# Stick-breaking attention in a hybrid decoder layer: carried sums folded to 64 rows, memory's norm taken by token, queries and keys split in 128 rows

## The chip, the cores and the metric

The kernel runs on one core of one Trainium2 chip. The metric is device time in microseconds (us) of one execution. The kernel before has a median of 851.5 us over three runs.

## The reference, cut to what matters

One layer, 512 tokens, width 1024, all in float32. The part that the change touches is the causal stick-breaking attention (8 heads of 64) and the norm of the 256 memory tokens:

```python
def rms_norm(x, g):
    var = jnp.mean(x * x, axis=-1, keepdims=True)
    return x * lax.rsqrt(var + EPS) * g

# stick-breaking attention: A[t,s] = sigmoid(z_ts) * prod_{s<j<t} (1 - sigmoid(z_tj)), z = q.k / sqrt(64), s < t
z = einsum('bhqd,bhkd->bhqk', qb, kb) * scale
log_fail = where(mask, log_sigmoid(-z), 0)
log_later = cumsum(log_fail, axis=3, reverse=True) - log_fail
weights = where(mask, exp(log_sigmoid(z) + log_later), 0)
out = einsum('bhqk,bhkd->bhqd', weights, vb)

# later, in the memory sublayer
m = rms_norm(mem, norm_mem_kv)          # 256 memory tokens
kv = m @ w_mem_kv
```

Around it stand the short convolution branch, the merge gates, the output projection, the memory cross-attention, a SwiGLU FFN and a final norm.

## The kernel before

Every product of float32 matrices is made of three products of float32r operands: an operand is split into a rounded part "hi" (a cast on ScalarE) and the remainder "lo" (a subtraction on VectorE), and hi*hi, hi*lo and lo*hi are added in PSUM (`mm3`, L154 to L156). A weight block of 128 columns is loaded by SyncE's queue into one of four `wr` buffers (L141), cast to `wh` (L149) and its remainder written to `wl` (L150). `gemm` then runs 24 matmuls of 512 columns.

**Attention.** Keys lie on partitions, queries on columns. The 8 heads are 4 pairs p; for each pair the key tiles kt = 3, 2, 1, 0 are swept (16 steps), with 128, 256, 384 and 512 query columns per head. `scores` (L408) makes z on TensorE, ScalarE makes softplus of it (Abs, Exp, Ln: L415 to L417; VectorE closes it, L418), GpSimd cuts the diagonal block (`causal`, L376), and the result e, the negative log of failing, is split in hi and lo (`l`, L390 and L391). e then gets the sum of all later key tiles added (L430) and is split once more (`r`): this running sum is carried into the next key tile. `weights` adds to z, in PSUM, first the carried sum (a matmul of each of the two parts of `r` with a 128x128 matrix of -1, L448) and then the sums inside the tile (parts of `l` with a triangle of -1, L451); ScalarE takes Exp (L453), GpSimd cuts the diagonal, VectorE scales and splits (`ah`, `al`, L457 and L458), and `values` multiplies with v (L470) one step later. For kt = 3 the carried sum is `l` itself and no `r` is made.

Between these pieces stands the filler: for each pair the projections of the next pair's q and k (`qk_part`), three projections of the convolution, and some gates, each one `gemm` of 24 matmuls. Scores of step i+1 are put in the middle of step i's filler; step i ends with `weights` of i and `values` of i-1. Some splits are deferred to the end of a step (`settle_behind`) and may not run before the last Exp of that step on ScalarE. A scheduler then sets the order of each engine's instructions, and each engine and each queue runs its own in order.

**q and k.** With two heads stacked on 128 partitions, k is held per head as hi in one half of the partitions and lo in the other; q is held per head as hi in both halves and lo in both halves. One matmul over 128 partitions then adds two of the products. Before, each half is cast and subtracted by itself (64 rows, L310, L313, L318, L322), and q's halves are copied across by four DMAs (L327).

**Memory's norm.** The transposed memory is loaded in four pieces during steps 1, 3, 5, 7 (L486), squared on ScalarE (L493), summed over its 8 tiles on GpSimd (L496, L498), split on VectorE (L184, L185), averaged over partitions by two matmuls (L190), and turned into the factors by a row of length 256 on ScalarE and VectorE; one row of it goes through DRAM on GpSimd's queue to give the same factors one per partition.

Of the kernel before, what the change touches and what calls it, by code (L numbers as in the profile page):

```python
# [21 lines left out]
MEM = 256  # L22
# [5 lines left out]
NJ = NF // 2  # L28
EPS = 1e-6
MEM_AT = (1, 3, 5, 7)  # L30
MEAN_AT = 13
EARLY = 2
WARM = 8
FIRST = 4
# [6 lines left out]


@with_exitstack
def hybrid_layer(ctx: ExitStack, tc: tile.TileContext, xT_d, memT_d, cols_d, wv_d, win_d,
                 wbr_d, wmix_d, wmq_d, wmk_d, wmv_d, wmo_d, wfi_d, wfo_d, gfin_d, out):
    nc = tc.nc

# [19 lines left out]
    def unit(s, cols=512):  # L67
        return upool.tile([P, cols], F32R, tag="u", name=nm(s), padded_shape=[P, 512])

    def tmp(s, cols=512):  # L70
        return tpool.tile([P, cols], F32, tag="t", name=nm(s), padded_shape=[P, 512])

    def f(ap):
        return ap.bitcast(F32)
# [228 lines left out]
        while behind:  # L303
            behind.pop(0)(*last)

    def qk_parts(p, i, t, last):
        if i:
            ks[p] = [unit("k") for _ in range(2)]
            for h, hs in enumerate(HALVES):
                casts.append(nc.scalar.copy(ks[p][h][hs, :], t[hs, :]))  # L310
                after(casts[-1], last)
            for h, hs in enumerate(HALVES):
                after(nc.vector.tensor_tensor(out=ks[p][h][HALVES[1 - h], :], in0=t[hs, :],  # L313
                                              in1=f(ks[p][h][hs, :]), op=ALU.subtract), last)
            return
        qs[p] = [[unit("q") for _ in range(2)] for _ in range(2)]
        for h, hs in enumerate(HALVES):
            casts.append(nc.scalar.copy(qs[p][h][0][hs, :], t[hs, :]))  # L318
            after(casts[-1], last)
        for h, hs in enumerate(HALVES):  # L320
            hi, lo = qs[p][h]
            after(nc.vector.tensor_tensor(out=lo[hs, :], in0=t[hs, :], in1=f(hi[hs, :]),  # L322
                                          op=ALU.subtract), last)
        for part in range(2):
            for h, hs in enumerate(HALVES):
                q = f(qs[p][h][part])
                nc.sync.dma_start(q[HALVES[1 - h], :], q[hs, :])  # L327

    gates = {}

# [54 lines left out]

    rest, later = {}, {}

    def lsplit(t, n, tag, bufs):
        hi, lo = (lpool.tile([P, n], F32R, tag=tag, name=nm(tag), bufs=bufs) for _ in range(2))
        nc.scalar.copy(hi, t)  # L390
        nc.vector.tensor_tensor(out=lo, in0=t, in1=f(hi), op=ALU.subtract)  # L391
        return hi, lo

    def part_of(parts, hs, some, n):

# [3 lines left out]
    def scores(p, kt):  # L399
# [11 lines left out]
        for hs, bank in zip(heads_of(kt), zs[p, kt]):  # L411
            w = len(hs) * n
            z = bank[:, :w]
            e = tmp("e")[:, :w]
            nc.scalar.activation(e, z, AF.Abs)  # L415
            nc.scalar.activation(e, e, AF.Exp, scale=-1.0)
            nc.scalar.activation(e, e, AF.Ln, bias=1.0)  # L417
            nc.vector.scalar_tensor_tensor(out=e, in0=z, scalar=0.0, in1=e, op0=ALU.max,  # L418
                                           op1=ALU.add)
            causal(by_head(e, n))  # L420
            bufs = 4 // len(hs)
            sp[p, kt, hs] = lsplit(e, w, f"l{kt}", bufs)
            if kt == TT - 1:
                later[hs] = e
                rest[p, kt - 1, hs] = sp[p, kt, hs]
            elif kt > 0:
                t = by_head(e, n)[:, :, P:]
                before = heads_of(kt + 1)[0] if len(heads_of(kt + 1)) == 1 else hs
                old = by_head(part_of([later[before]], before, hs, n - P)[0], n - P)
                nc.vector.tensor_tensor(out=t, in0=t, in1=old, op=ALU.add)  # L430
# [52 lines left out]
    accm = tmp("accm", MEM)  # L483

    def load_mem(k2, t):
        nc.sync.dma_start(t, memT_d[2 * k2 * P:(2 * k2 + 2) * P, :].rearrange("(j p) t -> p j t",  # L486
                                                                              p=P))

    def mem_square(k2):

        mk = f(unit("mk")).rearrange("p (j t) -> p j t", j=2)
        load_mem(k2, mk)
        nc.scalar.activation(mk, mk, AF.Square)  # L493
        for j in range(2):
            if k2 + j == 0:
                nc.gpsimd.tensor_copy(accm, mk[:, j, :])  # L496
            else:
                nc.gpsimd.tensor_tensor(out=accm, in0=accm, in1=mk[:, j, :], op=ALU.add)  # L498

    fill = []  # L500
    for p in range(TT):
# [804 lines left out]
def _layout(x, mem, norm_mix, w_in, conv_w, w_branch_a, w_branch_b, w_mix_out, norm_mem_q,  # L1306
# [12 lines left out]
    def by_pair(w):  # L1319
# [8 lines left out]
    arrays = {  # L1328
        "xT": x[0].T,
        "memT": mem[0].T,  # L1330
        "columns": columns.T,
        "w_value": by_row(w_in[0][:, O_V:O_V + SBW]),
        "w_in": by_column(w_in[0]),
# [30 lines left out]
```

## Time and profile before

| | |
|---|---|
| three runs | 851.5 us median, 851.43 to 852.21 |
| profiled execution | 850.78 us, its span 849.1 us, granted TensorE clock 0.998 |
| TensorE busy | 838.4 us, 99% of the span, 4778 matmuls in the trace |
| VectorE / ScalarE / GpSimd busy | 656.2 / 458.4 / 159.7 us |
| attention and its filler | about 28 to 196 us of the span |

The span runs from the first to the last instruction; the execution is 1.7 us longer. A matmul's row in the profile is longer than the distance to the next one, because matmuls are pipelined: the row's length includes the way through the array. What a matmul costs in a stream is therefore read from the starts of neighbouring rows, and a stall shorter than that tail shows as a larger distance of starts, not as idle time. PE is TensorE, DVE VectorE, ACT ScalarE, POOL GpSimd, SP SyncE, and a q behind a name is that engine's queue of DMA issues.

### The profile page before, as it was taken

How to read it: one execution, taken by the hardware profiler on the slowest of the kernel's cores; microseconds unless marked ns; L12 is line 12 of the kernel's file. 1: busy time of each engine (PE TensorE's matmuls, PEld its weight loads, DVE VectorE, ACT ScalarE, POOL GpSimd, SP SyncE). 2: the span in 40 equal slices, each digit the busy share in tenths (PEclk: the TensorE clock that was granted, in tenths of full speed). 3: DMA queues.
4: the chain of work that ended last, by engine and by line, in shares of the span. 5: the costliest groups of instructions: out<-in, count | busy, mean ns of one | idle time of the engine just before them, and what ended most of it. 6: DMA issues, size and time to landing. Idle time of an engine off the chain costs nothing.

```text
span 849.1 us, 12662 instructions
## 1 busy us (share of the span) xinstructions
PE 838.4 (99%) x4778; PEld 737.8 (87%) x4778; DVE 656.2 (77%) x1043; ACT 458.4 (54%) x810; POOL 159.7 (19%) x171
## 2 busy tenths in 40 slices
PE   9999999999999999999999999999999999999996
PEld 7888887888888899888888789999999999888885
DVE  7869989896766586587455679888887888999786
ACT  7567767474333344444444556655555555576664
POOL 0013221120566640163000101111111110000001
PEclk9999999999999999999999999999999999999999
DMA  8542232225588765566431335767767772465552
GB/s 298 156 142 64 93 117 75 75 76 183 200 310 309 297 245 190 174 230 247 151 81 49 112 75 142 181 174 187 186 176 187 190 186 85 155 221 196 171 187 99
DMA packets 50510, 141.62 MB, mean 167 GB/s; under 512 B 5521, under 2 KB 7569, under 8 KB 47634
## 3 DMA queue, kind: packets, MB, share of 16 engines
q1 hardware_dynamic: 40818, 105.93, 36.7%
q0 software_dynamic: 9344, 34.62, 15.7%
q8 instruction: 37, 0.61, 0.3%
q10 hardware_dynamic: 288, 0.28, 0.1%
q14 instruction: 23, 0.19, 0.1%
HBM read 125.07 MB, written 13.64 MB: 163 GB/s over the span
## 4 chain that ended last, share of the span: by engine, by line
PE 95%; DVE 3%; ACT 1%; issue 0%; DMA 0%; POOL 0%; SPq 0%; ACTq 0%
PE z L817 15%; PE p L1083 11%; PE y L817 7%; PE pr L154 7%; PE pr L155 7%; PE pr L156 7%; PE v L817 4%; PE r L156 3%; PE r L154 3%; PE r L155 3%; PE v L272 3%; PE mq L156 2%; PE mq L154 2%; PE br L155 2%; PE br L154 2%; PE mq L155 2%
## 5 line engine op out<-in xcount | busy, mean ns | idle before, releaser
L149 ACT CAST wh<-wr 128x1024 fp32r<-128x1024 f32 x84 | 88.0, 1052 | 151.7 <-issue 70.9
L150 DVE TENSOR_TENSOR wl<-wr,wh 128x1024 fp32r<-128x1024 f32 x84 | 110.6, 1318 | 37.0 <-ACT wh L149 36.9
L154 PE MATMUL pr<-xgh,wh 128*128 128x512 f32 x288 | 112.7, 391 | 0.0
L155 PE MATMUL pr<-xgl,wh 128*128 128x512 f32 x288 | 112.3, 390 | 0.0
L156 PE MATMUL pr<-xgh,wl 128*128 128x512 f32 x288 | 112.3, 390 | 0.0
L552 POOL TENSOR_TENSOR pre<-pre 128x512 f32<-128x512 f32 x44 | 72.1, 1642 | 31.4 <-DMA pre<-in_w_ffn_out_dram 29.1
L786 POOL DMA_DIRECT2D ws<-in_w_ffn_in_dram x22 | 26.5, 1207 | 258.4 <-DVE wf L807 104.7
L817 PE MATMUL z<-xdh,wf 128*128 128x256 f32 x352 | 70.5, 283 | 0.2 <-ACT sb L838 0.2
L156 PEld LDWEIGHTS pr<-xgh,wl 128*128 128x128 f32 x288 | 54.1, 188 | 11.5
L154 PEld LDWEIGHTS pr<-xgh,wh 128*128 128x128 f32 x288 | 54.1, 188 | 10.6
L155 PEld LDWEIGHTS pr<-xgl,wh 128*128 128x128 f32 x288 | 54.1, 188 | 10.3
L838 ACT COPY sa<-z 128x256 f32<-128x256 f32 x44 | 16.4, 373 | 79.2 <-PE z L817 79.1
L817 PEld LDWEIGHTS z<-xdh,wf 128*128 128x128 f32 x352 | 57.3, 189 | 0.5 <-ACT sb L838 0.4
L807 DVE TENSOR_TENSOR wf<-s,wf 128x512 fp32r<-128x512 f32 x44 | 30.3, 691 | 26.0 <-ACT wf L806 25.8
L817 PE MATMUL z<-xdl,wf 128*128 128x256 f32 x176 | 49.8, 283 | 0.0
L898 DVE TENSOR_TENSOR wl<-wr,wh 128x1024 fp32r<-128x1024 f32 x33 | 40.3, 1220 | 4.4 <-ACT wh L965 4.2
L965 ACT CAST wh<-wr 128x1024 fp32r<-128x1024 f32 x33 | 34.6, 1049 | 7.0 <-DMA wr<-sums 3.3
L817 PE MATMUL z<-xch,wf 128*128 128x256 f32 x176 | 35.4, 284 | 0.1
L817 PE MATMUL v<-xoh,wf 128*128 128x256 f32 x176 | 35.4, 283 | 0.0
L817 PE MATMUL y<-xch,wf 128*128 128x256 f32 x176 | 35.4, 283 | 0.0
L817 PE MATMUL z<-xf,wf 128*128 128x256 f32 x264 | 35.4, 283 | 0.0
L817 PE MATMUL y<-xoh,wf 128*128 128x256 f32 x176 | 35.3, 283 | 0.0
(337 smaller groups left out, 2403.3 us busy)
## 6 DMA issues: line engine op xcount, KB each, us to landing
wr<-in_w_in_dram SPq DMA_DIRECT2D x36, 512.0 KB, 3.3
pre<-in_w_ffn_out_dram POOLq DMA_DIRECT2D x11, 1024.0 KB, 8.0
sums<-pre POOLq DMA_DIRECT2D x11, 1024.0 KB, 5.0
ws<-in_w_ffn_in_dram SPq DMA_DIRECT2D x22, 512.0 KB, 3.7
wg<-in_w_ffn_in_dram SPq DMA_DIRECT2D x22, 512.0 KB, 4.0
ws<-in_w_ffn_in_dram POOLq DMA_DIRECT2D x22, 512.0 KB, 6.4
wr<-sums SPq DMA_DIRECT2D x22, 512.0 KB, 3.9
wr<-in_w_ffn_out_dram SPq DMA_DIRECT2D x16, 512.0 KB, 3.5
```

Of the source, the lines that this page charges most:

```text
L149: after(nc.scalar.copy(h2, raw), lead[-1:])
L150: lows.append(nc.vector.tensor_tensor(out=l2, in0=raw, in1=f(h2), op=ALU.subtract))
L154: nc.tensor.matmul(ps, a[0], b[0], start=start, stop=False, **kw)
L155: nc.tensor.matmul(ps, a[0], b[1], start=False, stop=False, **kw)
L156: nc.tensor.matmul(ps, a[1], b[0], start=False, stop=stop, **kw)
L552: nc.gpsimd.tensor_tensor(out=t[:, a, :], in0=t[:, a, :], in1=t[:, b, :], op=ALU.add)
L786: nc.gpsimd.dma_start(s13, a[:, 0:4:3, :], accum_op=ALU.add)
L807: nc.vector.tensor_tensor(out=w[:, 1, :], in0=raw, in1=f(w[:, 0, :]), op=ALU.subtract)
L817: nc.tensor.matmul(ps[:, :HS], a, b, start=i < 3 and k == 0 and j == 0, stop=k == KP - 1 and j == 2, skip_group_check=True)
L898: nc.vector.tensor_tensor(out=lo, in0=src, in1=f(hi), op=ALU.subtract)
L965: nc.scalar.copy(hi, raw)
L1083: nc.tensor.matmul(res[i][s2], a[:, ts], b, start=j == 0 and n == 0, stop=n == 2 and j == (BEHIND - 1 if (i, s2) == (5, 1) else NJ - 1))
```

## The change

Three edits. First, `rests`: the sum of the two halves of the partitions of e is taken before it is split. The carried matmul has -1 everywhere, so it only sums over partitions; the upper 64 rows are copied down by a DMA and added to the lower 64, the sum's hi goes to rows 0 to 63 and its lo to rows 64 to 127 of one tile, and one matmul instead of two carries it (for kt = 2 and 1; kt = 3 stays). It is deferred to the end of the step. Second, q and k of pairs 1 to 3 are cast and subtracted in full height, and DMAs move the halves (6 for q, 3 for k; the last ones overwrite what the first ones read). Third, the memory is loaded by token, ScalarE's square sums along the row, the factors are made on 128x2 numbers, and go through DRAM to be spread over all partitions. The place where this ends is step 9 instead of 13.

```diff
-MEAN_AT = 13
+MEAN_AT = 9
...
+    def qk_parts(p, i, t, last):
+        if p == 0:
+            return qk_halves(p, i, t, last)
+        low, high = HALVES
+        hi, lo, other = unit("qk"), unit("qk"), unit("qk")
+        casts.append(nc.scalar.copy(hi, t))
+        after(casts[-1], last)
+        after(nc.vector.tensor_tensor(out=lo, in0=t, in1=f(hi), op=ALU.subtract), last)
+        if i:
+            moves = (other, low, hi, high), (other, high, lo, high), (hi, high, lo, low)
+            ks[p] = [hi, other]
+        else:
+            rest = unit("qk")
+            moves = [(b, to, a, high) for a, b in ((hi, other), (lo, rest)) for to in HALVES]
+            moves += [(a, high, a, low) for a in (hi, lo)]
+            qs[p] = [[hi, lo], [other, rest]]
+        for a, to, b, at in moves:
+            nc.sync.dma_start(f(a)[to, :], f(b)[at, :])
...
+    def rests(p, kt, hs, e, w, last):
+        low, high = HALVES
+        t = tmp("rf")[:, :w]
+        nc.sync.dma_start(t[low, :], e[high, :])
+        nc.vector.tensor_tensor(out=t[low, :], in0=t[low, :], in1=e[low, :], op=ALU.add)
+        r = lpool.tile([P, w], F32R, tag=f"r{kt}", name=nm("r"), bufs=2 // len(hs))
+        after(nc.scalar.copy(r[low, :], t[low, :]), last)
+        nc.vector.tensor_tensor(out=r[high, :], in0=t[low, :], in1=f(r[low, :]), op=ALU.subtract)
+        rest[p, kt - 1, hs] = r,
...
                 later[hs] = e
-                rest[p, kt - 1, hs] = lsplit(e, w, f"r{kt}", bufs)
+                behind.append(lambda *last, e=e, w=w, hs=hs: rests(p, kt, hs, e, w, last))
...
-    def mem_square(k2):
-        mk = f(unit("mk")).rearrange("p (j t) -> p j t", j=2)
-        load_mem(k2, mk)
-        nc.scalar.activation(mk, mk, AF.Square)
-        for j in range(2):
-            if k2 + j == 0:
-                nc.gpsimd.tensor_copy(accm, mk[:, j, :])
-            else:
-                nc.gpsimd.tensor_tensor(out=accm, in0=accm, in1=mk[:, j, :], op=ALU.add)
+    def mem_square(i):
+        h, t = divmod(i, MT)
+        mk = f(unit("mk"))
+        nc.sync.dma_start(mk, mem_d[t, :, h * 512:(h + 1) * 512])
+        nc.scalar.activation(mk, mk, AF.Square, scale=D ** -0.5, accum_out=ms[:, i:i + 1])
+
+    def mem_factors():
+        var = spool.tile([P, MT], F32, tag="mv", name="mv", bufs=1)
+        nc.vector.tensor_tensor(out=var, in0=ms[:, :MT], in1=ms[:, MT:], op=ALU.add)
+        rm = rstd_of(var, MT, "rm")
+        d = dpool.tile([1, MEM], F32, tag="rm", name="rmd")
+        nc.gpsimd.dma_start(d.rearrange("o (t p) -> p (o t)", p=P), rm)
+        rmb = cpool.tile([P, MEM], F32, tag="rmb", name="rmb")
+        nc.gpsimd.dma_start(rmb, d.broadcast_to([P, MEM]))
+        return rm, rmb
...
-        if i == MEAN_AT - 4:
-            mean = squares_mean(accm, MT)
         if i == MEAN_AT:
-            rmb = mean[0]("rmb")
-            rm = turned_row(rmb[0:1, :], MT, "rm", nc.gpsimd, nc.gpsimd)
+            rm, rmb = mem_factors()
```

The scheduler moves instructions with it. In the rows below a number behind a name is a buffer's; line numbers of the changed kernel are its own (L478 is the former L448, L481 the former L451, L410 and L421 the former L391, L418 the new addition of the halves).

TensorE, pair 0, `weights` of kt = 1: z_611 and z_614 (now z_613 and z_616) are the two heads' scores, r the carried sum, l the tile's own. Before:

```order
L448 MATMUL z_611<-r_542,neg_91 128x256
L448 MATMUL z_611<-r_543,neg_91 128x256
L451 MATMUL z_611<-l_623,negtri 128x384
L448 MATMUL z_614<-r_542,neg_91 128x256
L448 MATMUL z_614<-r_543,neg_91 128x256
```

Now:

```order
L478 MATMUL z_613<-r_580,neg_91 128x256
L481 MATMUL z_613<-l_625,negtri 128x384
L481 MATMUL z_613<-l_626,negtri 128x384
L478 MATMUL z_616<-r_580,neg_91 128x256
L481 MATMUL z_616<-l_636,negtri 128x384
L481 MATMUL z_616<-l_637,negtri 128x384
```

One matmul per head takes the place of two, here and at kt = 0 of every pair.

VectorE, pair 2, from the convolution's product to the second half of the weights of kt = 2 (al_1491, now al_1499). Before:

```order
L348 TENSOR_TENSOR cu_1475<-pr_1450,r0b_363 128x512
L391 TENSOR_TENSOR r_1426<-e_1414,r_1425 128x384
L349 TENSOR_TENSOR cu_1475<-cu_1475,gc_1406 128x512
L391 TENSOR_TENSOR r_1441<-e_1429,r_1440 128x384
L351 TENSOR_SCALAR cv_1479<-cu_1475,gcol 128x512
L150 TENSOR_TENSOR wl_1726<-wr_1723,wh_1725 128x1024
L355 SCALAR_TENSOR_TENSOR cv_1479<-cu_1475,gcol,cv_1479 128x512
L457 TENSOR_SCALAR ah_1490<-a_1487,r_372 128x512
L355 SCALAR_TENSOR_TENSOR cv_1479<-cu_1475,gcol,cv_1479 128x512
L458 SCALAR_TENSOR_TENSOR al_1491<-a_1487,r_372,ah_1490 128x512
```

Now:

```order
L367 TENSOR_TENSOR cu_1483<-pr_1458,r0b_363 128x512
L150 TENSOR_TENSOR wl_1738<-wr_1735,wh_1737 128x1024
L368 TENSOR_TENSOR cu_1483<-cu_1483,gc_1422 128x512
L370 TENSOR_SCALAR cv_1487<-cu_1483,gcol 128x512
L374 SCALAR_TENSOR_TENSOR cv_1487<-cu_1483,gcol,cv_1487 128x512
L487 TENSOR_SCALAR ah_1498<-a_1495,r_372 128x512
L374 SCALAR_TENSOR_TENSOR cv_1487<-cu_1483,gcol,cv_1487 128x512
L488 SCALAR_TENSOR_TENSOR al_1499<-a_1495,r_372,ah_1498 128x512
L418 TENSOR_TENSOR rf_1508<-rf_1508,e_1430 64x384
L418 TENSOR_TENSOR rf_1514<-rf_1514,e_1441 64x384
L421 TENSOR_TENSOR r_1511<-rf_1508,r_1511 64x384
L448 SCALAR_TENSOR_TENSOR e_1545<-z_1539,e_1545 128x512
```

The two splits of the carried sum stood ahead of al; their additions and splits now stand behind it.

VectorE, a few instructions later in pair 2, where the weights of kt = 1 are split (heads 0 and 1). Before:

```order
L391 TENSOR_TENSOR l_1542<-e_1535,l_1541 128x512
L457 TENSOR_SCALAR ah_1567<-a_1564,r_372 128x384
L458 SCALAR_TENSOR_TENSOR al_1568<-a_1564,r_372,ah_1567 128x384
L457 TENSOR_SCALAR ah_1578<-a_1575,r_372 128x384
L458 SCALAR_TENSOR_TENSOR al_1579<-a_1575,r_372,ah_1578 128x384
L174 TENSOR_TENSOR yl_1587<-gb_1557,yh_1586 128x512
```

Now:

```order
L410 TENSOR_TENSOR l_1562<-e_1555,l_1561 128x512
L487 TENSOR_SCALAR ah_1586<-a_1583,r_372 128x384
L150 TENSOR_TENSOR wl_1804<-wr_1801,wh_1803 128x1024
L488 SCALAR_TENSOR_TENSOR al_1587<-a_1583,r_372,ah_1586 128x384
L487 TENSOR_SCALAR ah_1596<-a_1593,r_372 128x384
L448 SCALAR_TENSOR_TENSOR e_1632<-z_1627,e_1632 128x256
L488 SCALAR_TENSOR_TENSOR al_1597<-a_1593,r_372,ah_1596 128x384
```

A weight split (wl) and the next pair's softplus (e) now stand between the last l and the second head's al.

More of the change, by code (lines that the diff above doesn't have):

```diff
@@ L43, in hybrid_layer @@
 @with_exitstack
-def hybrid_layer(ctx: ExitStack, tc: tile.TileContext, xT_d, memT_d, cols_d, wv_d, win_d,
+def hybrid_layer(ctx: ExitStack, tc: tile.TileContext, xT_d, memT_d, mem_d, cols_d, wv_d, win_d,
                  wbr_d, wmix_d, wmq_d, wmk_d, wmv_d, wmo_d, wfi_d, wfo_d, gfin_d, out):
@@ L304, in settle_behind, with qk_halves @@
             behind.pop(0)(*last)
-    def qk_parts(p, i, t, last):
+    def qk_halves(p, i, t, last):
         if i:
@@ L386, in hybrid_layer, with lsplit @@
     rest, later = {}, {}
-    def lsplit(t, n, tag, bufs):
+    def lsplit(t, n, tag, bufs, last=()):
         hi, lo = (lpool.tile([P, n], F32R, tag=tag, name=nm(tag), bufs=bufs) for _ in range(2))
-        nc.scalar.copy(hi, t)
+        after(nc.scalar.copy(hi, t), last)
         nc.vector.tensor_tensor(out=lo, in0=t, in1=f(hi), op=ALU.subtract)
         return hi, lo
+    def rests(p, kt, hs, e, w, last):
[7 more added lines that the diff above has]
+        rest[p, kt - 1, hs] = r,
     def part_of(parts, hs, some, n):
@@ L481, in values @@
             oT.append(split(t, "o"))
-    accm = tmp("accm", MEM)
     def load_mem(k2, t):
@@ L487, in load_mem @@
                                                                               p=P))
[L489 to L498 removed]
+    ms = cpool.tile([P, 2 * MT], F32, tag="ms", name="ms")
+    def mem_square(i):
[12 more added lines that the diff above has]
+        return rm, rmb
     fill = []
@@ L1330, in _layout @@
         "memT": mem[0].T,
+        "mem": mem[0].reshape(MT, P, D),
         "columns": columns.T,
```

## The prediction

> **What bounds the kernel now.** I read the page's busy shares and its chain first, then the busy time by stretch (last row: stretch, its length, busy us of PE, PEld, DVE, ACT and POOL with their instructions, granted clock, DMA):
>
> ```profile
> PE 838.4 (99%) x4778; PEld 737.8 (87%) x4778; DVE 656.2 (77%) x1043; ACT 458.4 (54%) x810; POOL 159.7 (19%) x171
> PE 95%; DVE 3%; ACT 1%; issue 0%; DMA 0%; POOL 0%; SPq 0%; ACTq 0%
> 28.00:196.00 168.00, 167.04 (x791) 140.06 (x790) 141.71 (x231) 111.09 (x202) 36.90 (x62) 1.00 0.32 103
> ```
>
> TensorE is busy nearly everywhere, and 95% of the chain that ended last is TensorE. In the attention (28 to 196 us), the only stage that the change touches, it is busy 167.04 of 168 us. So a matmul that goes is worth its place in the stream, and an instruction on another engine costs only where TensorE comes to wait for it. VectorE, busy 141.71 of those 168 us, is the engine closest behind.
>
> "Busy" hides short stalls, since a matmul's row reaches 0.2 us past the start of the next one. So I went along the starts of TensorE's rows in the timeline of this stage and looked for distances over the usual one. The usual ones (two 256-column matmuls take 0.24 us of the stream, two of 384 take 0.35; one of 512 takes 0.23, the last two rows):
>
> ```profile
> 64.41 0.40 PE L448 MATMUL z<-r,neg 128*128 128x256 f32 x2
> 64.65 0.34 PE L451 MATMUL z<-l,negtri 128*128 128x384 f32 x1
> 77.76 0.51 PE L448 MATMUL z<-r,neg 128*128 128x384 f32 x2
> 78.11 0.62 PE L451 MATMUL z<-l,negtri 128*128 128x512 f32 x2
> 78.57 0.51 PE L448 MATMUL z<-r,neg 128*128 128x384 f32 x2
> ```
>
> And the places where TensorE really stood, in the same columns (start, length, what):
>
> ```profile
> 65.06 0.28 PE L470 MATMUL o<-ah,v 128*128 128x256 f32 x1
> 65.39 0.39 PE L470 MATMUL o<-al,v 128*128 128x256 f32 x1
> 122.98 0.40 PE L470 MATMUL o<-ah,v 128*128 128x512 f32 x1
> 123.32 0.50 PE L470 MATMUL o<-al,v 128*128 128x512 f32 x1
> 139.22 0.61 PE L408 MATMUL z<-q,k 128*128 128x512 f32 x2
> 140.37 0.73 PE L408 MATMUL z<-q,k 128*128 128x512 f32 x2 [0.53 <-ACT a L453]
> 140.94 0.39 PE L154 MATMUL pr<-xgh,wh 128*128 128x512 f32 x1
> 144.86 0.28 PE L470 MATMUL o<-ah,v 128*128 128x256 f32 x1
> 145.51 0.39 PE L470 MATMUL o<-al,v 128*128 128x256 f32 x1 [0.38 <-DVE al L458]
> ```
>
> Against those distances the first two rows lose 0.33 - 0.12 = 0.2 us, the next two 0.34 - 0.23 = 0.1 us; from 139.22 to 140.94 stand 1.72 us for four matmuls of 0.23, 0.8 us lost; from 144.86 to 145.51 0.65 us for one of 0.12, 0.5 us lost. In sum 1.6 us of stalls. All but the one at 139 stand ahead of a product with al, the last of VectorE's pieces.
>
> **What leaves TensorE.** The groups of the carried-sum matmul with two parts:
>
> ```profile
> L448 PE MATMUL z<-r,neg 128*128 128x384 f32 x16 | 4.1, 337 | 0.0
> L448 PE MATMUL z<-r,neg 128*128 128x256 f32 x16 | 3.2, 281 | 0.0
> ```
>
> The order of the changed kernel keeps one of each two: 8 of 384 columns at 0.35 / 2 = 0.175 us and 8 of 256 at 0.24 / 2 = 0.12 us go: 1.40 + 0.96 = 2.36 us. The length in the rows (337, 281 ns) would be the wrong price, for most of it lies under the next matmul. The Trainium skill (TensorE: Matmul & The Clock Gate, Back-to-back issue gap) gives a sustained spacing of 131 ns at 512 columns and 81 ns at 128; an estimate between them (98 and 114 ns) would make this term 1.7 us and the forecast 848.9. This trace does not agree: it shows 0.23 us at 512 columns, so that rule gets no weight in the sum.
>
> Memory's norm had two matmuls in the stream, with their waits around them:
>
> ```profile
> 168.88 0.39 PE L154 MATMUL pr<-xgh,wh 128*128 128x512 f32 x1
> 169.21 0.39 PE L190 MATMUL varb<-acch,mean_r 128*128 128x256 f32 x1
> 169.55 0.40 PE L155 MATMUL pr<-xgl,wh 128*128 128x512 f32 x1
> ```
>
> From 168.88 to 169.55 are 0.67 us where 0.23 would stand: 0.44 us go. Both together: **2.8 us off TensorE's stream**, all other matmuls staying.
>
> **What moves on the other engines, and what of it reaches TensorE.** Prices from the groups of the attention (count, busy us, mean ns) and the landing of q's copies:
>
> ```profile
> L322 DVE TENSOR_TENSOR q<-qk,q 64x512 fp32r<-64x512 f32 x8 | 5.5, 683 | 0.1
> L391 DVE TENSOR_TENSOR r<-e,r 128x384 fp32r<-128x384 f32 x8 | 4.7, 587 | 0.6 <-ACT r L390 0.6
> L391 DVE TENSOR_TENSOR r<-e,r 128x512 fp32r<-128x512 f32 x4 | 2.7, 678 | 0.2 <-ACT r L390 0.2
> L310 ACT CAST k<-qk 64x512 fp32r<-64x512 f32 x8 | 4.9, 618 | 0.1
> DMA to landing us min/median/max: 2.2/2.3/5.3
> ```
>
> 64 rows cost what 128 rows cost (683 against 678 ns). So full-height q and k save two of four VectorE operations and two of four casts per pair, for three pairs: 6 x 0.68 = 4.1 us of VectorE, 6 x 0.62 = 3.7 us of ScalarE. The fold adds one VectorE addition per carried sum, 4 of 512 and 8 of 384 columns: 4 x 0.68 + 8 x 0.59 = 7.4 us; its casts and subtractions stay in number and length. GpSimd loses the eight operations of memory's sum, VectorE six of 256 columns (at most 0.43 us each, the row of accl below: 2.6 us), and gets five on two columns, below that price. VectorE ends within 1 or 2 us of its old sum: how much does not decide, only where.
>
> Where it matters is pair 2, around the stalls at 139 and 145. The chain of waits there is VectorE's:
>
> ```profile
> 133.09 0.70 DVE k L313
> 133.81 0.43 DVE accl L185
> 139.80 0.47 DVE r L391
> 140.87 0.68 DVE r L391
> 144.72 0.75 DVE al L458
> ```
>
> Out of it go one of k's two subtractions (0.70), the memory's split (0.43), and the two r (1.15), which the new order puts behind al; into it come the addition and the subtraction of kt = 2's fold (2 x 0.68). That is 0.9 us less ahead of al. This stretch also began late:
>
> ```profile
> 118.52 1.99 POOL L498 TENSOR_TENSOR accm<-accm,mk 128x256 f32<-128x256 f32 x2 [2.07 <-ACT mk L493]
> 120.79 0.49 DVE L457 TENSOR_SCALAR ah<-a,r 128x512 fp32r<-128x512 f32 x1 [1.69 <-POOL a L376]
> ```
>
> The diagonal of pair 1's last weights waited behind two memory additions on GpSimd, and VectorE 1.69 us for it. Without them that start can come up to 1.69 us sooner; I take 1.3, since memory's square and two tiny steps now stand between ScalarE's pieces there. Against it TensorE itself reaches 139 us sooner: by 1.2 us of removed matmuls (two pairs) and by the two small stalls, 1.5 us in all. So the 1.3 us at 139 and 145 change by 1.5 - 0.9 - 1.3, to 0.6; those at 65 and 123 (0.3 us), which stand behind memory's square or additions, go. Bounds: none of the 1.6 us saved, all of it saved. I take 1.0 us saved.
>
> What comes new: behind al VectorE now does the two r and two additions, 4 x 0.59 = 2.4 us, then a weight split and an e, before the second head's next al:
>
> ```profile
> 151.84 0.62 DVE L458 SCALAR_TENSOR_TENSOR al<-a,r,ah 128x384 fp32r<-128x384 f32 x1
> 154.06 0.33 PE L470 MATMUL o<-al,v 128*128 128x384 f32 x1
> ```
>
> That al ended at 152.46; its matmul started at 154.06, 1.6 us later; the path to it is now longer and TensorE's need sooner. I charge 0.5 us, bounds 0 and 1.5.
>
> **Waits that come new.** The fold's copy waits on SyncE's queue for e, and behind it stand weight loads; k's and q's last copies wait until the first ones have landed (2.3 us), with the same loads behind them. A load and its cast are far apart:
>
> ```profile
> 59.15 0.34 SPq L141 DMA_DIRECT2D wr<-in_w_in_dram  x1
> 86.03 1.05 ACT L149 CAST wh<-wr 128x1024 fp32r<-128x1024 f32 x1 [0.59 <-PE pr L155]
> ```
>
> 27 us for this one, so two landings' time in the queue is hidden. On VectorE the addition waits for the copy's landing, with e, l and al queued behind it. The folded sum of pair 0, kt = 2 shows the room:
>
> ```profile
> 53.66 0.41 DVE L430 TENSOR_TENSOR e<-e,e 128x256 f32<-128x256 f32 x1
> 54.99 0.68 DVE L391 TENSOR_TENSOR r<-e,r 128x512 fp32r<-128x512 f32 x1
> ```
>
> e stands at 54.07, r was done at 55.67, and the first L448 that reads it starts at 64.41: 8.7 us, of which a copy (2.3) and an addition (0.68) take 3. In pairs 1 to 3 at least one gemm of 24 matmuls (5.4 us at 0.23) stands between as well. The row through DRAM moves to a place where GpSimd's next select is due; it holds GpSimd from the one DMA's issue to its landing. I count these waits at 0; the upper bound is the slower rival.
>
> **Sum.** -2.8 - 1.0 + 0.5 = -3.3 us. Against the profiled execution (850.78 us, span 849.1) that is 847.5. It ran 0.7 us under the median of 851.5, so the forecast for the median is **848.2 us**. What follows the attention keeps its order and its TensorE stream, so the gain should reach the end.
>
> **Rivals.** (1) VectorE swallows it: TensorE comes earlier to pair 2, but VectorE's pieces there do not, so that what was saved before 145 us (4 x 0.12 + 4 x 0.175 + 2 x 0.12 = 1.4 us) turns into longer waits for al and no stall is won: -2.8 + 1.4 = -1.4, 850.1 us. For it: the chain above is VectorE's from 133 to 145 us. Against it: the 1.69 us wait on GpSimd at its head goes. (2) Slower, by one mechanism: the copies land late and VectorE, in order, stands at the fold's addition while e, l and al queue behind. With a landing of 5.3 instead of 2.3 us it stands 3.0 us per pair of heads; it decides where two steps follow each other within a gemm or two (pairs 0 and 2): 2 x 3.0 = 6.0 us against 3.3, 854.2 us. It turns the sign once these waits exceed 3.3 us in all. For it: one copy of q did land in 5.3 us. Against it: the median is 2.3. (3) All stalls go and none comes: -2.8 - 1.6 = -4.4, 847.1 us. (4) The fold does not thin the stream, because TensorE's next operand is late anyway: the waits on TensorE (0.5 and 0.4 us named) are too few for that; it falls together with rival 1.
>
> **Chances and range.** Forecast 66%, rival 1 (with 4) 15%, rival 2 7%, rival 3 12%. A change of under 0.2% (1.7 us) cannot be told from none: forecast and rival 3 are faster, but for a small part of the forecast whose stalls come out on the bad side (none saved, 1.5 new: -1.3): faster 0.79; within 0.2% 0.14 (rival 1 without its worst end); slower 0.07. The range from 846.4 (rival 3 and 0.7 us, the spread of the runs) to 850.6 us (past rival 1) leaves out rival 2.
>
> **What would show it.** Right: 18 matmuls fewer; L478 with 16 folded matmuls, each followed at 0.12 or 0.175 us; the 1.99 us of GpSimd ahead of pair 1's last select gone; the distances around 65 and 123 us at their usual size; a smaller one at 139 and 145, a new one near 151. Wrong: VectorE idle ahead of `rf`, waiting for a DMA; al waits that add up to more than 1.6 us; or an idle TensorE at the start of a pair, waiting for q's or k's last copy.

## The result, and the profile after

| | before | changed |
|---|---|---|
| median | 851.46 us (851.07 to 852.21, 6 runs) | 858.19 us (856.72 to 859.65, 6 runs) |
| ratio | | 1.0078, 95% interval 1.0068 to 1.0088 |
| profiled execution, its span | 850.78, 849.1 us | 856.72, 855.0 us |
| matmuls in the trace | 4778 | 4760 |

The changed kernel is 6.7 us **slower**. The forecast was 848.2 us (846.4 to 850.6), and slower had a chance of 0.07.

First the page's busy shares and the attention's row of the busy time by stretch (stretch, length, busy us of PE, PEld, DVE, ACT and POOL, granted clock, DMA), as shown of before:

```profile
PE 838.3 (98%) x4760; PEld 737.0 (86%) x4760; DVE 656.9 (77%) x1048; ACT 455.2 (53%) x808; POOL 150.2 (18%) x163
28.00:196.00 168.00, 161.50 (x750) 135.31 (x749) 139.58 (x233) 104.98 (x196) 26.91 (x54) 0.98 0.37 112
```

Eighteen matmuls are gone, as announced, and TensorE is still as busy in sum (838.3 us), because some matmuls now last longer. In the attention it is busy 161.50 of 168 us where it was 167.04, and the clock's mean is 0.98 instead of 1.00. The groups of the folded matmul, and TensorE's rows at the two places that used to stall near 65 and 123 us:

```profile
L478 PE MATMUL z<-r,neg 128*128 128x384 f32 x8 | 2.7, 338 | 0.0
L478 PE MATMUL z<-r,neg 128*128 128x256 f32 x8 | 2.2, 277 | 0.0
65.39 0.28 PE L500 MATMUL o<-ah,v 128*128 128x256 f32 x1
65.50 0.28 PE L500 MATMUL o<-al,v 128*128 128x256 f32 x1
121.51 0.40 PE L500 MATMUL o<-ah,v 128*128 128x512 f32 x1
121.74 0.40 PE L500 MATMUL o<-al,v 128*128 128x512 f32 x1
```

The starts are 0.11 and 0.23 us apart: both stalls have gone, and up to here the run goes as predicted, about 1.6 us ahead of before. Then, in pair 2, TensorE's rows:

```profile
134.61 0.27 PE L500 MATMUL o<-al,v 128*128 128x128 f32 x1
139.26 0.79 PE L154 MATMUL pr<-xgh,wh 128*128 128x512 f32 x1 [4.38 <-DVE gc L361]
140.71 0.63 PE L154 MATMUL pr<-xgh,wh 128*128 128x512 f32 x1
141.99 0.63 PE L154 MATMUL pr<-xgh,wh 128*128 128x512 f32 x1
144.55 1.28 PE L438 MATMUL z<-qk,qk 128*128 128x512 f32 x4
149.34 0.28 PE L500 MATMUL o<-ah,v 128*128 128x256 f32 x1
149.94 0.39 PE L500 MATMUL o<-al,v 128*128 128x256 f32 x1 [0.33 <-DVE al L488]
155.12 0.66 PE L438 MATMUL z<-qk,qk 128*128 128x128 f32 x4 [1.79 <-ACT a L483]
```

TensorE stands for 4.5 us ahead of the convolution's gemm (L154); such idle time on TensorE is called a hole below. Then three matmuls take 1.28 us (140.71 to 141.99), 0.427 us each, where 0.23 is usual: from 139.26 to 144.55 twelve matmuls take 5.29 us instead of 2.76, which loses 2.5 us more. At 149.34 another 0.5 us and at 155.12 another 1.8 us are lost. The busy time by stretch shows the clock behind it:

```profile
134.60:139.20 4.60, 0.28 (x3) 0.14 (x2) 1.84 (x4) 1.69 (x4) 0.00 (x0) 0.88 0.51 153
139.20:144.50 5.30, 5.24 (x12) 4.13 (x13) 4.69 (x10) 4.54 (x9) 0.59 (x2) 0.50 0.41 127
```

The granted clock is 0.50 behind the hole; below, this is called the half clock. So 4.5 + 2.5 + 0.5 + 1.8 = 9.3 us are lost, and 2.8 us of matmuls and the 1.6 us of old stalls are won: +4.9 us. The span grew by 5.9 us; 1.0 us of it I cannot assign. Most of that lies behind the attention: the matmul of the carried sum at 189.10 us of before starts at 194.30 us now, 5.2 us later.

What TensorE waited for, followed back, begins on GpSimd. Its rows of that time, then the rows of SyncE's queue (start, length, what):

```profile
121.14 0.74 POOL L532 DMA_DIRECT2D rmd<-rm  x1 [3.43 <-DVE rm L129]
121.90 0.43 POOL L395 TENSOR_SCALAR_AFFINE_SELECT e<-e 128x256 f32<-128x256 f32 x1
129.66 0.57 POOL L534 DMA_DIRECT2D rmb<-rmd  x1 [7.33 <-DMA rmd<-rm]
130.24 0.42 POOL L395 TENSOR_SCALAR_AFFINE_SELECT a<-a 128x256 f32<-128x256 f32 x1
```

```profile
119.17 10.90 SPq L346 DMA_DIRECT2D qk<-qk  x6
130.16 2.38 SPq L141 DMA_DIRECT2D wr<-in_w_in_dram  x1
132.64 0.46 SPq L417 DMA_DIRECT2D rf<-e  x1
```

And the landing of q's and k's moves:

```profile
DMA to landing us min/median/max: 2.2/2.6/7.6
```

Two queues stand until the same moment. GpSimd holds `rmb` until `rmd`, issued at 121.14, has landed, and the select of pair 2's first weights waits behind it until 130.24. SyncE's queue holds the sixth of q's moves, which overwrites what the fourth reads, until the fourth has landed. The sixth was issued at 129.60 (119.17 + 10.90, less 0.46 us for one issue), 0.06 us from `rmb`, and behind it stand a weight load and the fold's copy. The next rows are VectorE's and ScalarE's behind these two queues:

```profile
130.69 0.35 DVE L487 TENSOR_SCALAR ah<-a,r 128x256 fp32r<-128x256 f32 x1 [6.67 <-POOL a L395]
137.80 0.68 DVE L418 TENSOR_TENSOR rf<-rf,e 64x512 f32<-64x512 f32 x1 [2.73 <-DMA rf<-e]
138.51 0.69 DVE L361 TENSOR_TENSOR gc<-pr,r0b 128x512 f32<-128x512 f32 x1
```

```profile
138.52 0.62 ACT L420 CAST r<-rf 64x512 fp32r<-64x512 f32 x1 [2.92 <-DVE rf L418]
```

VectorE stands 6.67 us for the select, and then 2.73 us for the copy, which was issued behind a weight load and lands only at 137.8, 5.1 us later. The drain of the projection's bank (`gc`) is queued behind the addition, and it is what TensorE's 4.38 us wait names.

### The profile page after: what moved, and what is told of

Same layout as the page of the kernel before. It is cut to its first block, busy times and chain, and to the rows that moved or that the text cites. A ratio compares the mean times of both kernels' runs of the same rounds, so it can differ in the third digit from the quotient of the medians.

```text
span 855.0 us, 12666 instructions
## 1 busy us (share of the span) xinstructions
PE 838.3 (98%) x4760; PEld 737.0 (86%) x4760; DVE 656.9 (77%) x1048; ACT 455.2 (53%) x808; POOL 150.2 (18%) x163
## 4 chain that ended last, share of the span: by engine, by line
PE 90%; DVE 4%; ACT 2%; issue 2%; DMA 1%; POOL 0%; SPq 0%; ACTq 0%; POOLq 0%
PE z L851 15%; PE p L1117 11%; PE y L851 7%; PE pr L154 6%; PE pr L156 6%; PE pr L155 6%; PE v L851 4%; PE r L155 3%; PE r L154 3%; PE r L156 3%; PE v L272 3%; PE br L154 2%; PE mq L156 2%; PE mq L154 2%; PE mq L155 2%; PE br L156 2%
## 5 line engine op out<-in xcount | busy, mean ns | idle before, releaser
L154 PE MATMUL pr<-xgh,wh 128*128 128x512 f32 x288 | 113.8, 395 | 4.4 <-DVE gc L361 4.4
L154 PEld LDWEIGHTS pr<-xgh,wh 128*128 128x128 f32 x288 | 54.7, 190 | 15.3 <-DVE gc L361 4.5
```

Of the source, the lines that this page charges most:

```text
L154: nc.tensor.matmul(ps, a[0], b[0], start=start, stop=False, **kw)
```

## The experiments

Each run was compared with runs of the kernel before on the same chip (medians 851.5 to 852.1 us). "Late" means that a DMA of GpSimd stands behind the attention's last select.

| run | what runs | median us | ratio (95%) |
|---|---|---|---|
| e1 | the change, `rmb` late | 856.51 | 1.0051 (1.0039 to 1.0064) |
| e2 | fold, full-height q and k; old norm | 855.90 | 1.0048 (1.0033 to 1.0064) |
| e3 | norm by token alone | 856.28 | 1.0054 (1.0040 to 1.0068) |
| e4 | fold alone | 855.54 | 1.0047 (1.0033 to 1.0060) |
| e5 | the change, `rmd` and `rmb` late | 848.64 | 0.9967 (0.9955 to 0.9980) |
| e6 | norm alone, both late | 849.42 | 0.9970 (0.9958 to 0.9981) |
| e7 | fold alone, no copy | 853.56 | 1.0017 (1.0008 to 1.0026) |
| e8 | e5, halves copied by ScalarE | 849.44 | 0.9971 (0.9960 to 0.9982) |
| e9 | the change, idle time filled with zeros | 861.18 | 1.0106 (1.0090 to 1.0121) |
| e10 | fold and norm, both late; q, k by halves | 855.78 | 1.0046 (1.0034 to 1.0059) |
| e11 | norm, both late, full-height q and k; no fold | 850.08 | 0.9980 (0.9971 to 0.9989) |
| e12 | e5, halves copied by GpSimd | 848.61 | 0.9966 (0.9953 to 0.9979) |
| e13 | the change, `rmd` in pieces of 8 bytes | 853.79 | 1.0024 (1.0013 to 1.0035) |
| e14 | the change, idle time filled at full height | 863.89 | 1.0146 (1.0126 to 1.0166) |

### e1 to e4: one wait removed, and the parts apart

e1 moves the second DMA behind the sweep:

```diff
-        nc.gpsimd.dma_start(rmb, d.broadcast_to([P, MEM]))
+    # behind the loop over the steps
+        after(nc.gpsimd.dma_start(rmb, d.broadcast_to([P, MEM])), last_selects)
```

> The changed kernel with one move: the second DMA of memory's factors (rmb, DRAM to 128 partitions) stands on GpSimd behind the attention's last select instead of ahead of a select of pair 2; the first one (rmd) stays. Theory A (GpSimd stands 7.3 us at rmb for rmd's landing, and everything from 130 to 160 us follows from it): the new stalls go with it, some 10 us of TensorE's starts, and the time is 848.2 us as forecast, 847.2 to 849.5. Theory B (the fold's copies through SP's queue land late by themselves, 5.1 us behind a weight load, and VectorE stands at them): the stall before the convolution's gemm of pair 2 stays at 3 us or more, 853 to 858 us. Theory C (q's and k's moves): the wait of z on qk's softplus at 155 us stays, 1.9 us, and the time is 850 to 851.

It took 856.51 us: of the 6.7 us lost, 1.9 came back (4.85 us over its own before). Theory A, that GpSimd's wait is the whole cause, fell. The time lies in theory B's range; whether B's cause, copies that are late by themselves, is the right one, e5 decides. The trace of e1 (SyncE's queue, then the waits of that stretch, in us in total, times, longest):

```profile
119.40 11.22 SPq L346 DMA_DIRECT2D qk<-qk  x6
```

```profile
DVE rf L421 <- DMA rf<-e: 8.3, 1, 8.3
```

GpSimd no longer stands, but SyncE's queue does, and VectorE now waits 8.3 us for the fold's copy. Two paths led from the same moment to the same place; taking away one showed the other.

e2 has the fold and the full-height q and k with the old norm; e4 the fold alone on the kernel before; e3 the norm alone on the kernel before (the diffs are the parts of the change).

> Fold and full-height q and k, with memory's norm as it was before. Theory A: nothing holds GpSimd; -2.4 us of matmuls, without the 0.44 us of the norm's matmuls and with the old stalls at 65, 123, 139 and 145 us (1.6 us) partly left: 849.5 us, 848.6 to 850.6. Theory B: as slow as the whole change, 854 to 858 us.

> The kernel before with memory's norm by token alone (its two DMAs at step 9). Theory A: GpSimd stands some 7 us for rmd's landing ahead of pair 2's first weights; VectorE comes late to the pieces of pair 2, without a copy to wait for, and TensorE stands for about 2 us more than before there: 853 us, 852 to 857; slower than before. Theory B: no copies, so no loss: 850.7 to 851.3 us.

> The kernel before with the fold alone. Theory A: -2.4 us of matmuls, the old stalls left, VectorE with 7.4 us more of additions: 849.6 us, 848.8 to 851. Theory B: VectorE stands at late copies, 853 to 858 us.

All three are slower than before, by 3.9 to 4.6 us. e3 did what theory A said, as GpSimd's row and TensorE's longest wait in the attention show:

```profile
131.01 0.57 POOL L504 DMA_DIRECT2D rmb<-rmd  x1 [7.96 <-DMA rmd<-rm]
PE z L408 <- ACT a L453: 3.9, 1, 3.9
```

In e2 and e4 neither `rmd` nor its wait exists, and I had expected 849.5 us. Their times lie in theory B's range. e4's rows of VectorE, ScalarE and TensorE in pair 1:

```profile
106.88 1.01 DVE L399 TENSOR_TENSOR rf<-rf,e 64x384 f32<-64x384 f32 x2
107.45 0.51 ACT L401 CAST r<-rf 64x384 fp32r<-64x384 f32 x1 [5.70 <-DVE rf L399]
113.66 0.55 PE L419 MATMUL z<-q,k 128*128 128x128 f32 x3 [2.43 <-ACT a L464]
```

The copies land in 2.0 to 2.9 us there, so theory B's late landing is not it either. ScalarE stands 5.70 us at the cast of the folded sum, because e, its copy and VectorE's addition come one after the other, and the softplus of the next tile and the Exp are queued behind that cast; TensorE then waits 2.43 us for a bank. The copy is only a part of this wait: the two heads' copies had landed at 104.80 and 106.20 us, and VectorE, which is not idle there, came to their additions at 106.88. So the fold has a stall of its own in the kernel before. In e2, too, ScalarE stands at the cast of r (1.90 us at 147 us) ahead of TensorE's longest hole, of 2.5 us at 152 us.

### e5 and e6: both of memory's DMAs late

```diff
-        nc.gpsimd.dma_start(d.rearrange("o (t p) -> p (o t)", p=P), rm)
+    # behind the loop over the steps, ahead of rmb
+        after(nc.gpsimd.dma_start(d.rearrange("o (t p) -> p (o t)", p=P), rm), last_selects)
```

> The changed kernel with both of memory's DMAs (rmd, rmb) behind the attention's last select on GpSimd; every other engine's order is that of the changed kernel, row for row. Theory D (revised): the scattered write rmd, 8.2 us under way from 121 us on, makes q's and k's moves land in 7.6 to 7.9 us (2.6 the median) while it lasts, SyncE's queue stands at the last of them until 130 us, and the fold's copy and with it VectorE and ScalarE start late; without it nothing stands, and the time is 848.5 us, 847.4 to 850.0. Theory E: the fold's copy stalls TensorE by its own round trip, at an ordinary landing, as in the run of the fold alone (ScalarE idle for 5.7 us ahead of the cast of r, TensorE for 2.4): 852 to 856 us.

e5 takes 848.64 us and is faster than before. All other instructions stand in the same order on every engine, so the place of these two DMAs is worth 10.2 us (from +6.7 to -3.5 against before), and the place of `rmd` alone 8.3 (from e1's +4.85). The rows of e5: the attention's stretch, SyncE's queue, the landing of q's and k's moves, TensorE's only wait in the attention, and GpSimd's late row:

```profile
28.00:196.00 168.00, 166.85 (x787) 140.38 (x786) 145.60 (x241) 110.45 (x203) 26.84 (x53) 1.00 0.42 119
```

```profile
119.98 4.83 SPq L346 DMA_DIRECT2D qk<-qk  x6
```

```profile
DMA to landing us min/median/max: 2.2/2.6/3.4
```

```profile
PE z L441 <- ACT a L486: 1.2, 1, 1.2
```

```profile
199.04 0.57 POOL L541 DMA_DIRECT2D rmb<-rmd  x1 [10.53 <-DMA rmd<-rm]
```

The six moves take 4.83 us of the queue instead of 10.90, the slowest move that the view tells lands in 3.4 us instead of 7.6, the clock is 1.00, and GpSimd's wait, now 10.53 us, is where nobody stands behind it that TensorE needs. The fold's copy that landed in 5.1 us in the change (4.4 in e1) lands in 3.8. Theory D holds.

> The kernel before with memory's norm by token, both of its DMAs behind the attention's last select; all else in the order of the run of the norm alone. Theory D: the 3.9 us wait of z at 144 us goes, with the half clock behind it; -0.44 us of matmuls and part of the old 1.6 us of stalls: 850.3 us, 849.3 to 851.2. If the place of the squares and not the DMAs did it: 854 us and more.

e6 is the kernel before with the norm by token and late DMAs. It takes 849.42 us, 2.7 us less than its before and better than I expected. All other instructions stand in e3's order, so the place of the two DMAs is worth 7.3 us here. Its attention has no stall left:

```profile
28.00:196.00 168.00, 168.00 (x800) 142.12 (x799) 142.88 (x234) 113.61 (x209) 28.04 (x53) 1.00 0.35 105
```

### e7, e10, e11: what the fold needs

e7 leaves the copy out:

```diff
-        nc.sync.dma_start(t[low, :], e[high, :])
-        nc.vector.tensor_tensor(out=t[low, :], in0=t[low, :], in1=e[low, :], op=ALU.add)
+        nc.vector.tensor_tensor(out=t[low, :], in0=e[low, :], in1=e[low, :], op=ALU.add)
```

> The fold alone without its copy: the addition adds the lower 64 rows to themselves, so the upper rows are left out of the carried sum; all instructions but the 12 DMAs stay, though the order shifts by some places. Theory E: the round trip of the DMA is what ScalarE stands for, and without it the 2.4 us matmuls are won: 849.3 us, 848.4 to 850.5. Theory F (VectorE's 7.4 us of additions make the pieces late, whatever the copy): 853 to 856 us.

e7 takes 853.56 us, 1.5 us over its before: 2.4 us better than the fold alone, and still slower than before. The round trip is at most a part of the loss; the time lies in theory F's range. e7's attention and its largest waits on TensorE:

```profile
28.00:196.00 168.00, 163.91 (x765) 135.64 (x764) 150.35 (x244) 111.54 (x203) 31.62 (x62) 1.00 0.31 98
```

```profile
PE z L461 <- DVE l L391: 2.8, 3, 1.5
```

VectorE is busy 150.35 us of 168, and TensorE waits for its pieces. Since the order shifted with the copy, this run alone does not separate the two cleanly. e10 and e11 do it in e5's frame: e10 keeps q and k by halves, e11 has no fold.

```diff
 e10: qk_parts
-        if p == 0:
+        if p < 9:
             return qk_halves(p, i, t, last)
 e11: scores
-                behind.append(lambda *last, e=e, w=w, hs=hs: rests(p, kt, hs, e, w, last))
+                rest[p, kt - 1, hs] = lsplit(e, w, f"r{kt}", bufs)
```

> Fold and memory's norm, both of its DMAs late; q and k by halves as before. If q's and k's moves ahead of the fold's copy on SyncE's queue cause the 1.3 us that were left at 145 us in the run with both DMAs late: 847.5 us, 846.8 to 848.4. If the fold's own additions and casts cause it (VectorE has 4.1 us more without the full-height q and k): 849 to 850.5 us.

> Memory's norm with both DMAs late and full-height q and k, without the fold. No matmul more goes than in the run of the norm alone with late DMAs (849.4 us), which has no stall left: 849.4 us, 848.6 to 850.2. If the fold's 2.4 us were all lost to its stalls: at or below the run with fold (848.6).

Against their own runs of before: norm alone -2.7 us (e6), with full-height q and k -1.7 (e11), with the fold +4.0 (e10), with both -3.5 (e5). So the fold costs 6.7 us where VectorE still splits q and k by halves, and wins 1.8 us where it does not. The loss is clear of the noise; the gain is not, for the intervals of e5 and e11 overlap. Both were measured beside the late norm: e2 has the full-height split and the fold with the old norm, and is 4.2 us slower than before. e10's attention and longest wait:

```profile
28.00:196.00 168.00, 163.15 (x765) 135.72 (x764) 146.78 (x243) 111.44 (x206) 28.40 (x53) 1.00 0.34 104
```

```profile
PE z L441 <- ACT a L486: 3.9, 3, 2.5
```

My first guess for e10 (847.5 us, q's and k's moves in the queue are what is left) was wrong by 8 us; the alternative (849 to 850.5 us) was too low by 5 us. VectorE's 4.1 us, its cause, can be part of this; e10 also moves q by other DMAs, and which of the two weighs more stays open. The full-height split by itself wins nothing that these runs can tell (e11 against e6).

### e8 and e12: the halves moved by an engine

```diff
-        nc.sync.dma_start(t[low, :], e[high, :])
+        nc.scalar.copy(t[low, :], e[high, :])          (e8)
+        nc.gpsimd.tensor_copy(t[low, :], e[high, :])   (e12)
```

> The changed kernel with both of memory's DMAs late, as above, and the halves moved by ScalarE (12 copies of 64 rows, about 0.6 us each, 6.8 us of ScalarE's time) instead of by DMAs. Theory D and E: no landing stands in any engine's order any more but q's and k's: 848.0 us, 847.0 to 849.5. Theory F: 852 to 856 us.

> The changed kernel with both of memory's DMAs late and the halves moved by GpSimd (12 copies of 64 rows) instead of DMAs. If the 1.3 us left at 145 us are the copy's way through SyncE's queue and its landing (0.8 us of VectorE's wait, 2.4 of ScalarE's): 847.5 us, 846.8 to 848.5. If GpSimd's copy takes as long as the DMA's landing, or delays its selects: 848.5 to 850.5.

They take 849.44 and 848.61 us, no better than e5, where VectorE waits 2.1 us in all for the copies. The stall at 145 us shrinks by 0.2 to 0.4 us, and one of 1.2 us (e8) or 0.7 us (e12) comes at 186 us. So moving the halves without a DMA won nothing. In both kernels other instructions changed places with the copies, so this does not show that the copy's way is free. e5 and e12 are the fastest versions that were run, 0.33 and 0.34% under before.

### e13: the number of pieces

```diff
-        nc.gpsimd.dma_start(d.rearrange("o (t p) -> p (o t)", p=P), rm)
+        nc.gpsimd.dma_start(d.rearrange("o (p t) -> p (o t)", p=P), rm)
```

> The changed kernel with memory's two factors of a partition written side by side, so that rmd goes in 128 pieces of 8 bytes instead of 256 of 4; place and order of every instruction stay. The row's order is thereby another than the one that is read (the memory keys' factors are mixed up). Theory K (the number of pieces makes the landing): half the time under way, 4 to 5.5 us instead of 8.2, GpSimd's wait and the landing of q's and k's moves shorter by about 3 to 4 us, the idle time of TensorE at 139 us from 4.5 to about 1 us, without the half clock: 850 to 853 us. Theory L (the place, among the other transfers, makes it): 7 to 9 us under way, 857 to 859 us.

e13 takes 853.79 us, 2.1 us over its before. So 4.6 us of the change's loss are gone, with every instruction in its place in the order: only the pieces of `rmd` differ, 128 of 8 bytes in place of 256 of 4. e13's DMA issues (KB, median us to landing) and GpSimd's row:

```profile
rmd<-rm POOLq DMA_DIRECT2D x1, 1.0 KB, 3.4
```

```profile
125.26 0.57 POOL L534 DMA_DIRECT2D rmb<-rmd  x1 [2.68 <-DMA rmd<-rm]
```

The same 1 KB lands in 3.4 us instead of 8.2, and GpSimd stands 2.68 us instead of 7.33. Theory K holds against L, though its lower bound of 4 us for the landing was still too high. The pieces' number and their size changed together; this run does not part the two. The time lies 0.8 us over K's range, and the trace has a hole of 2.0 us at 150 us with the half clock behind it, which K did not count on. The sixth of q's moves starts at 125.21 us, again 0.05 us from `rmb`: the landing that it waits for comes with `rmd`'s here too.

### e9 and e14: the half clock

e9 puts matmuls that add zeros into the hole, so that they change nothing but the work of the array (the call is shortened here):

```diff
+        for _ in range(64):
+            nc.tensor.matmul(ops[2][1][:, 3 * P:], neg1[:HD, :], zeros_of_negtri, start=False, ...)
```

> The changed kernel with 64 matmuls that add zeros (64 rows, 128 columns) to an output bank, between the first values of pair 2 and the gemm that stood idle for 4.5 us: TensorE works through the hole instead of standing, everything else waits as before. Theory G: the half clock (0.50 from 139 to 144 us, 427 ns a matmul) follows from the idle time; kept busy, the gemm runs at 0.23 us each and 2.5 to 2.9 us come back: 855.5 us, 854.5 to 856.5. Theory H: the half clock comes from something else in this stretch (its operands, the traffic): 857.5 to 859 us, as the changed kernel.

Neither number came. TensorE's row of the fill and a stretch in it:

```profile
135.87 10.98 PE L515 MATMUL o<-negtri,neg 64*128 64x128 f32 x64
```

```profile
139.20:142.00 2.80, 2.80 (x16) 2.80 (x14) 1.33 (x3) 0.65 (x2) 0.00 (x0) 0.50 0.38 80
```

TensorE was never idle and its clock fell to 0.50 all the same: the fill's matmuls start 0.11 us apart up to 139.1 us and 0.21 us apart from there on. The fill took 10.98 us and ended late. So work of this kind (64 of 128 rows, zeros) did not hold the clock.

> As the run with added zeros, but 40 matmuls of full height with no zero in their operands (they add a constant to an output bank, so pair 2's output is falsified), in the hole of 4.5 us. At 0.1 us each they take 4 us. Theory G (the clock halves when TensorE's array has had little to do for some 4 us, whether it stood or added zeros in half its rows): the clock stays at 1.00 in the gemm behind them, 855.5 us, 854.5 to 856.5. Theory H (it halves for another reason): 0.50 again, 857.5 us and more.

TensorE's row of this fill, then the stretch of the gemm behind it and a later one:

```profile
135.84 4.63 PE L515 MATMUL o<-neg 128*128 128x128 f32 x40
```

```profile
142.20:145.30 3.10, 3.01 (x13) 2.52 (x14) 2.87 (x5) 2.35 (x6) 0.33 (x2) 1.00 0.48 122
148.00:152.00 4.00, 4.00 (x12) 3.20 (x11) 3.93 (x7) 0.00 (x0) 0.02 (x1) 0.59 0.42 126
```

With 40 matmuls of full height and no zeros, the gemm behind them ran at clock 1.00, although another hole, of 2.0 us, lay between. That is what theory G said of this place. G's "some 4 us" does not hold: from 147.9 us on, behind the next hole, of 2.0 us, the clock was 0.50 again, and once more behind a hole of 3.6 us at 160 us. Whether the height or the zeros made the difference between e9 and e14 was not run. The time did not fall: the fill moved VectorE's order by some places, the gemm began at 142.29 us instead of 139.26, later waits grew, and two stretches of half clock followed. What the half clock alone costs is therefore read from the trace (2.5 us), not from this run.

## Why the prediction was wrong, step by step

**The step that failed** is in "Waits that come new": "The row through DRAM moves to a place where GpSimd's next select is due; it holds GpSimd from the one DMA's issue to its landing. I count these waits at 0". The hold was seen and not priced, and the upper bound that the prediction names for it, the slower rival, prices late copies of the fold and not this wait. The rows of before that come nearest are the old row's two DMAs (KB, median us to landing):

```profile
row<-rmb POOLq DMA_DIRECT2D x1, 1.0 KB, 1.6
rm<-row POOLq DMA_DIRECT2D x1, 1.0 KB, 2.5
```

The first writes 1 KB from one partition to DRAM; the second reads it back in 256 pieces of 4 bytes. No row of before writes such pieces. `rmd` does, and it measured 8.2 us (11.0 in e5, where it is late). Behind it stood the select, and behind the select pair 2's first weights.

**A second part of the same step** was too narrow: "behind it stand weight loads; k's and q's last copies wait until the first ones have landed (2.3 us), with the same loads behind them", and the loads have 27 us. The loads do. But the fold's copy stands in the same queue, and it has no such room. With `rmd` under way two of the moves took 8.4 and 7.6 us instead of 2.3, and the copy stood behind them.

**Slack was measured to the wrong reader.** The 8.7 us of the prediction are the time from the end of the old r (55.67 us) to the first L448. The cast of r, however, stands in ScalarE's order ahead of the next tile's softplus, and e4 shows ScalarE standing there for 5.70 us. "VectorE ends within 1 or 2 us of its old sum: how much does not decide, only where" is half right: e10, where VectorE does not get its 4.1 us back, stands 7.5 us behind e5, each against its own before.

**What no term held** is the clock: the long hole was followed by matmuls at half speed, which added 2.5 us to its 4.5.

**What was right.** The 18 matmuls (16 folded and 2 of the norm) went; their price of 2.8 us was not measured by itself. The 1.99 us of GpSimd ahead of pair 1's last select and the stalls at 65 and 123 us went. In e5, the change without its misplaced DMAs, those at 139 and 145 us went too, 1.6 us in all instead of 1.0, and a new one of 1.3 us came at 145 us (0.5 charged, bounds 0 and 1.5), though not as a wait for al: ScalarE stands at the cast of r. -2.8 - 1.6 + 1.3 = -3.1 us; measured against its before, -3.5: 848.64 us where 848.2 was forecast. The sum was that of a change with these DMAs out of the way. That it came so near is in part luck: 0.6 us more were won than it counted and 0.8 us more lost, by another wait than the one it charged; and without the full-height split (e10) or with the old norm (e2) the rest of the change is slower than before.

**The rivals.** Rival 2 described the picture that came (the copy lands in 5.1 us, VectorE stands at the addition, slower) and was given 7%. The first sign of being wrong that the prediction named, VectorE idle ahead of `rf` for a DMA, came (2.73 us). Copies that land late by themselves are not the cause: with `rmd` gone no copy of the fold lands later than 3.9 us, and VectorE waits 2.1 us for all twelve. Its price, 854.2 us, lacked the clock. Rivals 1 and 3 did not occur; e5's -3.5 us lies next to the forecast's -3.3.

## What to carry to other kernels

When a DMA is moved on a queue, ask what its landing holds, in how many pieces it goes, and what stands behind every instruction that waits for it or for its neighbours: a transfer of 1 KB cost 8.3 us by its place alone (e1 against e5). A part that loses time beside one set of companions need not lose it beside another (the fold: +6.7 us, and -1.8 us, which is not clear of the noise), so the parts of a change are to be timed in the frame in which they stay. And a hole on TensorE is to be priced with the slow matmuls that may follow it.

## What the runs showed of the hardware

- **A scattered write to DRAM is slow.** 256 pieces of 4 bytes landed in 8.2 to 8.9 us in the middle of the attention (the change, e1, e3) and in 10.2 to 12.2 us at its end (e5, e6, e12); 128 pieces of 8 bytes landed in 3.4 us (e13). The old row, 1 KB from one partition, landed in 1.6 us, and reading it back in 256 pieces of 4 bytes took 2.5 us.
- **It holds up landings of another queue.** In the change, the fourth of q's moves on SyncE's queue was issued with `rmd` (121.16 and 121.14 us) and the fifth 1 us later; they landed at 129.55 and 129.72 us, just behind `rmd` (129.37). The third, issued 0.5 us before `rmd`, landed in 2.2 us. The trace counts a landing in 16 steps: each of the fourth move's steps came 0.16 to 0.21 us behind one of `rmd`'s, from the first (124.65 and 124.81 us) to the last, in the change and in e1. The Trainium skill (DMA: Bandwidth & Descriptors, Queues, rings and completion order) says that a DMA engine's write of the completion count lands only after all earlier writes of that engine, of whatever queue. The trace agrees, with these pairs of steps; that this rule is the mechanism was not tested by itself.
- **The clock after a hole.** With holes of 4.5, 3.7 and 4.0 us (the change, e1, e3), of 2.5 and 2.6 us (e2, e4) and of 2.0 us (e13, e14) came a stretch of half clock, in which 512-column matmuls start 0.427 us apart. It lasted 3.41 us, in the change 6.83, and began between 1.2 us before the hole's end (the change) and 1.6 us behind it (e2). Behind holes of 2.7 us (e10), 2.0 us (e14, at 142 us) and 1.9 us (the change, at 155 us) none came: between 2.0 and 2.7 us the length alone does not decide. Executions of one kernel differ, too: e10's profiled one had a mean clock of 0.997 and took 854.1 us, its four others 0.994 to 0.995 and 855.5 to 856.9 us. The Trainium skill (TensorE: Matmul & The Clock Gate, Part 1: The HAM clock gate) gives half rate after an idle window of about 3.4 us that runs freely, and 426.7 ns for such a matmul. The 427 ns and the stretches' length agree; holes shorter than its window sufficed here four times. Zeros in half the rows did not hold the clock (e9), work at full height did, as far as the next hole (e14).
